# Third and fourth pair of the first group on POOL, and another pair order in down's first column groups

## The chip, the cores and the metric

The kernel runs on one core of one Trainium2 chip, in one launch. The metric is the device time of the program in microseconds (us), lower is better; the kernel before was run three times (2105.24, 2107.07 and 2103.96 us, median 2105.24). Profiles are taken by the hardware profiler from one execution. The engines are PE (TensorE), DVE (VectorE), ACT (ScalarE), POOL (GpSimd) and SP (SyncE, which here only issues DMAs).

## The reference

One layer of a streaming encoder on a residual stream x of 256 rows by 2048 columns, float32:

```python
x = x + 1/2 * SwiGLU_1(RMSNorm(x))     # d_ff 5504
h = RMSNorm(x); P = h @ W_in           # one combined projection
m = sigmoid(g_gdn) * (gated_deltanet(P) @ W_A) + sigmoid(g_att) * (chunk_attention(P) @ W_B)
x = x + m @ W_out
x = x + 1/2 * SwiGLU_2(RMSNorm(x))

def swiglu(h, w_gate, w_up, w_down):
    return (jax.nn.silu(h @ w_gate) * (h @ w_up)) @ w_down
```

Nearly all of the time is in matrix products of the 256 rows with weights that are read once from memory, 408 MB in all. The two SwiGLU blocks (gate and up, then down) hold the largest share of them.

## The kernel before, in words

Every float32 number is held as a high part (rounded by a cast to the PE's type fp32r) and a low part (the rest), and every product is three matmuls: high by high, high by low, low by high (lines 455, 456 and 457, in `product`). Weights come by DMA as f32 (`raw`, two DMAs of 512 KB for one pair), ACT casts the high part (`wh`, line 373) and DVE subtracts for the low part (`wl`, line 427). PE's matmuls name what they read, so "pf<-wl,xr" is the product with the low weights.

The work goes by pairs of k tiles (256 rows of a weight). Function `seven` computes one column group from eight pairs. A pair is either plain (24 matmuls) or fast: seven products in place of eight for the 2x2 blocks of a pair (21 matmuls), for which DVE first makes four sums of weight blocks (`s`, lines 399 to 401), ACT casts them (`sh`, line 406) and DVE subtracts (`sl`); the blocks that are used as they are become `w` and `v` (line 404). A fast pair so costs PE three matmuls less and DVE three times as much as a plain one. Its products go to seven banks in PSUM, numbered by bits (1, 2, 3, 4, 5, 6, 7, 8 in the names, "pd_00_4"); at the end of a column group they are added into four results, copied out (`ed`, lines 524 to 537) and, for down, added to the residual in memory by a DMA from POOL's queue (line 621).

Weights are planned ahead as one list (`plan`); `take_weights` draws from it in the order in which the products use them, and the order of the instructions on each engine is set by the scheduler of the framework from the order in the code. The order on each engine is fixed when the program is built, and an engine works through its own queue in that order.

Two places matter here. In the first column group of the first FFN, x itself arrives while the weights do. The pairs come in the order FIRST = 1, 3, 5, 7, 0, 2, 4, 6; pairs 1, 3, 5 and 7 are plain, the others fast in later groups. `feed(s)` runs ahead of step s: it loads x of pair FIRST[s+2], scales x of pair FIRST[s+1] by the norm's weight and splits it (`Xr.plain`: per pair two scalings with a cast on ACT, line 180, and two subtractions on DVE, line 181), and at given steps calls `stand(k4)`: eight transposes of x on PE (line 1142), two copies from PSUM, squares for the norm, and a store of the rows to memory (`put`, line 649).

The other place is down (hidden to 2048 columns). For two of the three chunks of each FFN, the 16 k tiles of the chunk are eight pairs, and `seven` runs them in order 0 to 7 for two column groups of 1024 columns (d = 0 and d = 2); pairs 2, 3, 5 and 6 (DEEP) are fast, so that 2 and 3 and later 5 and 6 stand side by side. Two chunks in each of two FFNs make four such places.

## Time and profile before

| | |
|---|---|
| median of three runs | 2105.24 us (2103.96 to 2107.07) |
| the profiled execution | 2104.86 us |
| its span in the trace | 2103.1 us |
| PE busy | 2086.8 us, 99% of the span |
| DVE, ACT, POOL busy | 1798.9, 1190.7 and 64.5 us |
| mean granted TensorE clock | 0.999 |
| memory read, written | 407.72 MB, 25.17 MB |

The span is what the profiler sees from the first to the last instruction; the run's own time is 1.8 us longer. PE is busy nearly throughout, so a time can only get shorter where PE idles or works slowly. The profile lists for each group of instructions the idle time just before it and what ended that time; such an entry on PE is the place to look.

### The profile page before, as it was taken

To read this page: it belongs to the slowest core of one execution; us is meant where nothing else is said; L and a number is where in the kernel's file an instruction comes from. 1 tells how busy PE (TensorE), PEld (TensorE's weight loads), DVE (VectorE), ACT (ScalarE), POOL (GpSimd) and SP (SyncE) were. 2 spreads that over 40 slices of the span, in tenths; PEclk is the share of its full clock that TensorE was granted. 3 is DMA by queue.
4 is the path that set the end of the run, shared out by engine and by line. 5 is a ranking of instruction groups with operands and counts; after the bars stand their busy time and mean duration, and the time that the engine had idled before them with its cause. 6 is when DMAs were issued, how large, how long until landed. Compare 5 with 4: busy or idle time off the path is not lost.

```text
span 2103.1 us, 25704 instructions
## 1 busy us (share of the span) xinstructions
PE 2086.8 (99%) x9732; PEld 1743.5 (83%) x9732; DVE 1798.9 (86%) x2015; ACT 1190.7 (57%) x1226; POOL 64.5 (3%) x77
## 2 busy tenths in 40 slices
PE   8999999999999999999999999999999999999999
PEld 6888888878898988888888888888887888878897
DVE  6998999989996688767785787999999999989982
ACT  6755565646555555557545555556555555556561
POOL 0000110002000000000010000000000100011000
PEclk9999999999999999999999999999999999999999
DMA  9655995649866656435454466767665975579581
GB/s 314 218 188 177 261 266 196 207 145 278 257 212 219 238 187 224 163 127 197 145 175 159 151 200 220 230 203 228 207 193 169 276 243 192 180 207 294 188 271 60
DMA packets 398204, 434.59 MB, mean 207 GB/s; under 512 B 14704, under 2 KB 372352, under 8 KB 397824
## 3 DMA queue, kind: packets, MB, share of 16 engines
q1 hardware_dynamic: 388864, 416.17, 60.8%
q0 software_dynamic: 9216, 16.78, 4.5%
q8 instruction: 76, 1.25, 0.3%
q14 instruction: 48, 0.39, 0.1%
HBM read 407.72 MB, written 25.17 MB: 206 GB/s over the span
## 4 chain that ended last, share of the span: by engine, by line
PE 95%; DVE 2%; SPq 1%; issue 1%; DMA 0%; ACT 0%; DVEq 0%; ACTq 0%
PE pf L455 14%; PE pf L457 14%; PE pf L456 14%; PE pd L456 7%; PE pd L457 7%; PE pd L455 7%; PE pg L456 2%; PE pg L457 2%; PE pg L455 2%; PE pc L455 2%; PE pc L457 2%; PE pc L456 2%; PE pwo L455 1%; PE pwo L457 1%; PE pwo L456 1%; DVE wl L427 1%
## 5 line engine op out<-in xcount | busy, mean ns | idle before, releaser
L427 DVE TENSOR_TENSOR wl<-raw,wh 128x2048 fp32r<-128x2048 f32 (+5 forms) x278 | 587.2, 2120 | 69.6 <-PE pc L456 17.0
L373 ACT CAST wh<-raw 128x2048 fp32r<-128x2048 f32 (+5 forms) x278 | 490.2, 1779 | 95.3 <-DVE wl L427 18.3
L406 ACT CAST sh<-s 128x2048 fp32r<-128x2048 f32 (+1 forms) x123 | 233.0, 1894 | 292.5 <-DVE s L401 288.4
L427 DVE TENSOR_TENSOR sl<-s,sh 128x2048 fp32r<-128x2048 f32 (+1 forms) x123 | 276.9, 2257 | 27.3 <-PE pd L456 12.0
L456 PE MATMUL pf<-wl,xr 128*128 128x512 f32 (+1 forms) x704 | 271.4, 386 | 0.2 <-DVE wl L427 0.2
L457 PE MATMUL pf<-wh,xr 128*128 128x512 f32 (+1 forms) x704 | 271.0, 385 | 0.0
L455 PE MATMUL pf<-wh,xr 128*128 128x512 f32 (+1 forms) x704 | 263.3, 387 | 3.9 <-ACT xr L180 2.4
L457 PE MATMUL pd<-wh,hid 128*128 128x512 f32 x432 | 169.1, 391 | 0.0
L456 PE MATMUL pd<-wl,hid 128*128 128x512 f32 x432 | 168.3, 390 | 0.0
L404 ACT CAST w<-raw 128x1024 fp32r<-128x1024 f32 (+1 forms) x123 | 128.0, 1041 | 65.4 <-DVE sl L427 12.8
L455 PE MATMUL pd<-wh,hid 128*128 128x512 f32 x432 | 163.6, 392 | 0.0
L455 PEld LDWEIGHTS pf<-wh,xr 128*128 128x128 f32 x704 | 132.4, 188 | 30.3 <-ACT wh L373 2.9
L427 DVE TENSOR_TENSOR w<-raw,w 128x1024 fp32r<-128x1024 f32 (+1 forms) x123 | 148.1, 1204 | 10.4 <-ACT w L404 10.2
L399 DVE TENSOR_TENSOR s<-raw 128x1024 f32<-128x1024 f32 (+1 forms) x123 | 147.9, 1202 | 7.1 <-PE pg L456 4.6
L456 PEld LDWEIGHTS pf<-wl,xr 128*128 128x128 f32 x704 | 132.6, 188 | 25.3 <-DVE wl L427 0.5
L457 PEld LDWEIGHTS pf<-wh,xr 128*128 128x128 f32 x704 | 132.6, 188 | 25.3
L404 ACT CAST v<-raw 128x512 fp32r<-128x512 f32 (+1 forms) x123 | 75.6, 615 | 97.0 <-PE pf L457 32.3
L456 PE MATMUL pf<-sl,xf 128*128 128x512 f32 (+1 forms) x292 | 112.3, 385 | 0.0
L457 PE MATMUL pf<-sh,xf 128*128 128x512 f32 (+1 forms) x292 | 112.0, 385 | 0.0
L455 PE MATMUL pf<-sh,xf 128*128 128x512 f32 (+1 forms) x292 | 110.2, 386 | 0.0
L621 POOL DMA_DIRECT2D xd<-ed x64 | 56.0, 996 | 1305.5 <-ACT ed L524 1225.5
L457 PEld LDWEIGHTS pd<-wh,hid 128*128 128x128 f32 x432 | 81.1, 188 | 17.2
(509 smaller groups left out, 4270.5 us busy)
## 6 DMA issues: line engine op xcount, KB each, us to landing
raw<-wd SPq DMA_DIRECT2D x168, 512.0 KB, 5.2
raw<-wg SPq DMA_DIRECT2D x159, 512.0 KB, 3.8
raw<-wu SPq DMA_DIRECT2D x159, 512.0 KB, 5.3
raw<-wgt SPq DMA_DIRECT2D x64, 512.0 KB, 4.6
raw<-wa SPq DMA_DIRECT2D x48, 512.0 KB, 4.6
raw<-wc SPq DMA_DIRECT2D x48, 512.0 KB, 4.7
xd<-ed POOLq DMA_DIRECT2D x64, 256.0 KB, 7.0
raw<-wbr SPq DMA_DIRECT2D x32, 512.0 KB, 5.2
```

Source lines behind the costliest of these rows:

```text
L373: nc.scalar.copy(hi, src)
L399: nc.vector.tensor_sub(S[:, 0:2], R[:, 1], R[:, :, 0])
L404: nc.scalar.copy(hi, src)
L406: nc.scalar.copy(sh, s)
L427: nc.vector.tensor_sub(lo, src, f32(hi))
L455: nc.tensor.matmul(dst, ah, wh, start=start, stop=False)
L456: nc.tensor.matmul(dst, ah, wl, start=False, stop=False)
L457: nc.tensor.matmul(dst, al, wh, start=False, stop=stop)
L621: b: lambda e, dst=xd[d + dd][t]: nc.gpsimd.dma_start(dst, e, accum_op=ALU.add)
```

## The change

Three things change. In the first group, x of the third and fourth pair (5 and 7) is scaled and split by a new function `Xr.pool` on POOL: two multiplications of 128x256, a cast of 128x512 and a subtraction of 128x512 for each pair, through a scratch tile `xa`. The steps in which `stand` is called each move one later, those of the last two falling together: steps 5, 6, 7 and 7 in place of 4, 5, 6 and 7. And down's first column groups (d = 0) take their pairs in the order APART = 0, 1, 2, 4, 3, 7, 5, 6, in the plan of the weights as in `seven`; the fast ones are still 2, 3, 5 and 6.

```diff
@@ -32,6 +32,7 @@
 DOWN = (2, 4, 6)
 SECOND = (1, 3, 0, 2, 4, 5, 6, 7)
 DEEP = (2, 3, 5, 6)
+APART = (0, 1, 2, 4, 3, 7, 5, 6)
 FIRST = (1, 3, 5, 7, 0, 2, 4, 6)
 QUAD = {2: (0, 0), 3: (1, 0), 4: (0, 1), 8: (1, 1)}
 CHUNKS = ((0, 4), (4, 8), (8, 11))
@@ -180,6 +181,16 @@
                 nc.scalar.activation(hi, src(i), AF.Copy, scale=self.w(j, i))
                 nc.vector.scalar_tensor_tensor(lo, src(i), self.w(j, i), f32(hi), op0=ALU.mult, op1=ALU.subtract)
 
+        def pool(self, j, src):
+
+            b = self.place(j)
+            a = wide(f"xa{self.nm}{j}").rearrange("p (b x) -> p b x", x=P)
+            for i in range(2):
+                to = a[:, 2 * i : 2 * i + 2].rearrange("p t x -> p (t x)")
+                nc.gpsimd.tensor_scalar_mul(to, src(i), self.w(j, i))
+            nc.gpsimd.tensor_copy(b[:, 0, 0:4], a)
+            nc.gpsimd.tensor_sub(b[:, 1, 0:4], a, f32(b[:, 0, 0:4]))
+
         def scale(self, j, src, a):
             for i in range(2):
                 nc.scalar.activation(
@@ -285,10 +296,11 @@
                     for j, p in zip(js, gu):
                         yield j in fast_pairs(f, i), p
                 k0, k1 = FG[a0][0], sum(FG[a1 - 1])
-                cols = lambda d: t_pieces(a["wd" + f], 4 * d, 4, k0, k1)
+                cols = lambda d, js=None: t_pieces(a["wd" + f], 4 * d, 4, k0, k1, js and [k0 + 2 * j for j in js])
                 if down_pairs(a0, a1):
                     for d in (0, 2):
-                        yield from sevens(cols(d), cols(d + 1), DEEP)
+                        js = range(KD // 2) if d else APART
+                        yield from sevens(cols(d, js), cols(d + 1, js), DEEP, js)
                 else:
                     for d in range(4):
                         yield from twos(cols(d))
@@ -300,8 +312,8 @@
         for p in pieces:
             yield False, (p, next(pieces))
 
-    def sevens(one, two, fast=DOWN):
-        for j, pieces in enumerate(zip(one, two)):
+    def sevens(one, two, fast=DOWN, pairs=range(KD // 2)):
+        for j, pieces in zip(pairs, zip(one, two)):
             yield j in fast, pieces
 
     def mixing():
@@ -621,7 +633,7 @@
                         b: lambda e, dst=xd[d + dd][t]: nc.gpsimd.dma_start(dst, e, accum_op=ALU.add)
                         for b, (dd, t) in QUAD.items()
                     }
-                    seven(f"d{nm}_{a0}{d}", 512, fast, block, out=out)
+                    seven(f"d{nm}_{a0}{d}", 512, fast, block, pairs=range(KD // 2) if d else APART, out=out)
                 continue
             for d in range(4):
                 pd = pair(f"pd{nm}_{a0}{d}")
@@ -1156,7 +1168,7 @@
     def feed(s):
 
         if s < 7:
-            xr1.plain(FIRST[s + 1], pair_of_x(FIRST[s + 1]))
+            (xr1.pool if 0 < s < 3 else xr1.plain)(FIRST[s + 1], pair_of_x(FIRST[s + 1]))
         if s < 6:
             load_x(2 * FIRST[s + 2], 2)
         if s == 1:
@@ -1166,7 +1178,7 @@
         if s > 1 and FIRST[s] in xr1.fast:
             xr1.more(FIRST[s], pair_of_x(FIRST[s]))
         for k4 in range(4):
-            if s == max(3, *(FIRST.index(2 * k4 + i) for i in range(2))):
+            if s == min(7, 1 + max(*(FIRST.index(2 * k4 + i) for i in range(2)))):
                 stand(k4)
         if s == 7:
             xr1.finish()
```

What this does to the queues, at three places. ACT in the first group of the kernel before, from the weights of the third pair on; `wh_191` is the fourth pair's high weights, `xr_5_196` holds x of the third and then of the fourth pair, `xT` is x as loaded:

```order
L373 CAST wh_168<-raw_126 128x1024 x2
L373 CAST wh_191<-raw_158 128x2048
L180 ACTIVATE xr_5_196<-xT_81,vec 128x256 x2
L373 CAST wh_218<-raw_165 128x2048
L180 ACTIVATE xr_5_196<-xT_81,vec 128x256 x2
L373 CAST wh_237<-raw_188 128x2048
```

And after the change, ACT, and then POOL at its start:

```order
L385 CAST wh_168<-raw_126 128x1024 x2
L385 CAST wh_191<-raw_158 128x2048
L385 CAST wh_219<-raw_165 128x2048
L385 CAST wh_238<-raw_188 128x2048
L385 CAST wh_263<-raw_216 128x2048
L181 ACTIVATE xf_0_279<-xT_80,vec 128x256 x2
```

```order
L190 ISA
L190 TENSOR_SCALAR xa_197<-xT_81,vec 128x256 x2
L191 CAST xr_5_196<-xa_197 128x512
L192 TENSOR_TENSOR xr_5_196<-xa_197,xr_5_196 128x512
L190 TENSOR_SCALAR xa_242<-xT_81,vec 128x256 x2
L191 CAST xr_5_196<-xa_242 128x512
L192 TENSOR_TENSOR xr_5_196<-xa_242,xr_5_196 128x512
```

The two scalings of `xr_5_196` have left ACT, where each stood between two casts of weights, and stand on POOL with nothing but each other; the two subtractions on DVE have gone as well.

DVE in down's first column groups (first FFN, first chunk) before. `wl_1646` is pair 4's low weights; `sl_1554` and the rows of number 1545 belong to fast pair 3, `s`, `v` and `w` with 1691 to 1693 to fast pair 5:

```order
L427 TENSOR_TENSOR sl_1554<-s_1545,sh_1553 128x2048
L145 TENSOR_TENSOR shid_3_1579_0_1615<-shid_3_1579_0_1615,hid_3_1579_0_0_1608 128x128
L146 TENSOR_TENSOR shid_3_1579_0_1615<-shid_3_1579_0_1615,hid_3_1579_0_0_1608 128x128
L147 TENSOR_TENSOR shid_3_1579_0_1615<-hid_3_1579_0_0_1608,shid_3_1579_0_1615 128x128
L148 TENSOR_TENSOR shid_3_1579_0_1615<-hid_3_1579_0_0_1608,shid_3_1579_0_1615 128x128
L427 TENSOR_TENSOR v_1693<-raw_1542,v_1693 128x512
L129 TENSOR_TENSOR hs_25_1255<-shid_3_1579_0_1615,hs_25_1255 128x512
L399 TENSOR_TENSOR s_1691<-raw_1542 128x1024
L427 TENSOR_TENSOR w_1692<-raw_1542,w_1692 128x1024
L400 TENSOR_TENSOR s_1691<-s_1691,raw_1542 128x512
L401 TENSOR_TENSOR s_1691<-raw_1542,s_1691 128x512
L427 TENSOR_TENSOR wl_1646<-raw_1488,wh_1645 128x2048
```

And after the change. `wl_1548` is pair 4's low weights, `s_1639`, `w_1640` and `sl_1648` belong to fast pair 3:

```order
L146 TENSOR_TENSOR shid_3_1573_0_1609<-shid_3_1573_0_1609,hid_3_1573_0_0_1602 128x128
L147 TENSOR_TENSOR shid_3_1573_0_1609<-shid_3_1573_0_1609,hid_3_1573_0_0_1602 128x128
L148 TENSOR_TENSOR shid_3_1573_0_1609<-hid_3_1573_0_0_1602,shid_3_1573_0_1609 128x128
L149 TENSOR_TENSOR shid_3_1573_0_1609<-hid_3_1573_0_0_1602,shid_3_1573_0_1609 128x128
L130 TENSOR_TENSOR hid_3_1573<-hid_3_1573_2_0_1629,hid_3_1573 128x2x256
L130 TENSOR_TENSOR hs_25_1257<-shid_3_1573_0_1609,hs_25_1257 128x512
L411 TENSOR_TENSOR s_1639<-raw_1490 128x1024
L412 TENSOR_TENSOR s_1639<-s_1639,raw_1490 128x512
L439 TENSOR_TENSOR w_1640<-raw_1490,w_1640 128x1024
L413 TENSOR_TENSOR s_1639<-raw_1490,s_1639 128x512
L439 TENSOR_TENSOR wl_1548<-raw_1452,wh_1547 128x2048
L439 TENSOR_TENSOR sl_1648<-s_1639,sh_1647 128x2048
```

Pair 4's subtraction has moved ahead of `sl` of pair 3, and the sums of pair 5 no longer stand in front of it.

ACT at the end of the same column groups before, from the first casts for the next column group on (`ed_00_2` to `ed_00_8` are the copies of banks 2, 3, 4 and 8; `v` and `w` with 1843, 1844, 1870 and 1871 are weights of d = 2):

```order
L524 COPY ed_00_0_1823<-pd_00_1_1663 128x512
L373 CAST wh_1835<-raw_1753 128x2048
L404 CAST v_1844<-raw_1795 128x512
L537 COPY ed_00_2_1896<-pd_00_2_1580 128x512
L404 CAST v_1871<-raw_1832 128x512
L537 COPY ed_00_3_1900<-pd_00_3_1594 128x512
L404 CAST w_1843<-raw_1795 128x1024
L537 COPY ed_00_4_1904<-pd_00_4_1584 128x512
L537 COPY ed_00_8_1908<-pd_00_8_1598 128x512
L406 CAST sh_1850<-s_1842 128x2048
```

And after the change (1885, 1886 and 1901 are weights of d = 2):

```order
L385 CAST wh_1789<-raw_1709 128x2048
L385 CAST wh_1831<-raw_1757 128x2048
L536 COPY ed_00_0_1856<-pd_00_1_1663 128x512
L416 CAST v_1886<-raw_1786 128x512
L416 CAST w_1885<-raw_1786 128x1024
L416 CAST v_1901<-raw_1828 128x512
L549 COPY ed_00_2_1866<-pd_00_2_1574 128x512
L549 COPY ed_00_3_1870<-pd_00_3_1588 128x512
L549 COPY ed_00_4_1874<-pd_00_4_1578 128x512
L549 COPY ed_00_8_1878<-pd_00_8_1592 128x512
```

The copies of the four banks are still behind two casts of `v`; banks 2 and 3 no longer have a cast between them.

## Rows read from the trace of the kernel before

**Rows 1.** The page's part 1: busy time of each engine, its share of the span and its instructions.

```profile
span 2103.1 us, 25704 instructions
...
PE 2086.8 (99%) x9732; PEld 1743.5 (83%) x9732; DVE 1798.9 (86%) x2015; ACT 1190.7 (57%) x1226; POOL 64.5 (3%) x77
```

**Rows 2.** What PE waited for over the whole span: us in total, times, the longest one.

```profile
PE pd L455 <- ACT sh L406: 3.7, 4, 0.9
PE pf L455 <- ACT xr L180: 2.4, 1, 2.4
```

**Rows 3.** PE by the time, end of the second and start of the third pair of the first group: start us, duration us, engine, line, operation, names, shapes, count, and in brackets the idle time before it with what ended it.

```profile
18.62 0.39 PE L457 MATMUL pf<-wh,xr 128*128 128x512 f32 x1
21.42 0.72 PE L455 MATMUL pf<-wh,xr 128*128 128x512 f32 x1 [2.41 <-ACT xr L180]
...
24.93 0.41 PE L457 MATMUL pf<-wh,xr 128*128 128x512 f32 x1
```

**Rows 4.** The first group in stretches of 5 us: busy time and instructions of PE, PEld, DVE, ACT and POOL, then the granted TensorE clock, the DMA share and GB/s.

```profile
20.00:25.00 5.00, 3.58 (x9) 2.84 (x10) 3.08 (x3) 3.66 (x4) 0.00 (x0) 0.66 1.09 359
...
30.00:35.00 5.00, 4.70 (x23) 3.65 (x22) 1.48 (x1) 2.09 (x3) 0.00 (x0) 1.00 1.09 355
```

**Rows 5.** ACT by the time in the first group, columns as in rows 3.

```profile
19.06 1.90 ACT L373 CAST wh<-raw 128x2048 fp32r<-128x2048 f32 x1 [2.72 <-DMA raw<-wu]
20.86 0.90 ACT L180 ACTIVATE xr<-xT,vec 128x256 fp32r<-128x256 f32 x2
22.06 1.90 ACT L373 CAST wh<-raw 128x2048 fp32r<-128x2048 f32 x1 [0.29 <-DMA raw<-wu]
25.65 0.91 ACT L180 ACTIVATE xr<-xT,vec 128x256 fp32r<-128x256 f32 x2 [1.70 <-DMA xT<-x]
...
34.56 0.91 ACT L180 ACTIVATE xf<-xT,vec 128x256 fp32r<-128x256 f32 x2 [2.91 <-DMA xT<-x]
```

**Rows 6.** The load of x for the third pair, which SP issues at 7.83 us (line 84): its time to landing; then the chain of waits at the fifth pair: start, us, what.

```profile
DMA to landing us min/median/max: 8.1/8.1/8.1
...
24.39 10.09 DMA xT<-x
```

**Rows 7.** DVE by the time in the first group.

```profile
22.20 2.28 DVE L427 TENSOR_TENSOR wl<-raw,wh 128x2048 fp32r<-128x2048 f32 x1
...
27.00 4.49 DVE L427 TENSOR_TENSOR wl<-raw,wh 128x2048 fp32r<-128x2048 f32 x2
```

**Rows 8.** PE by the time, end of the fourth pair, the first eight transposes and the fifth pair.

```profile
33.83 0.39 PE L457 MATMUL pf<-wh,xr 128*128 128x512 f32 x1
34.52 1.09 PE L1142 MATMUL xs<-cst,xT 128*128 128x128 f32 x8 [0.30 <-DMA xT<-x]
35.37 0.48 PE L455 MATMUL pf<-wh,xf 128*128 128x512 f32 x1
```

**Rows 9.** POOL's own computing, by the time, in the mixing stage.

```profile
1075.93 1.81 POOL L966 MEMSET gdn_pk<- 128x2048 f32 x1 [544.44 <-DVE wl L427]
1077.81 0.43 POOL L968 COPY gdn_pk<-gdn_E 32x256 f32<-32x256 f32 x1
...
1095.39 0.61 POOL L968 COPY gdn_pk<-gdn_E 64x512 f32<-64x512 f32 x1
```

**Rows 10.** DVE beside the second of those rows.

```profile
1077.79 0.19 DVE L976 TENSOR_TENSOR gdn_ls<-gdn_lw,gdn_ls 128x16 f32<-128x16 f32 x1
```

**Rows 11.** PE by the time in down's first column groups, first FFN, first chunk.

```profile
208.03 1.07 PE L455 MATMUL pd<-wh,hid 128*128 128x512 f32 x4
...
209.16 0.39 PE L456 MATMUL pd<-w,hid 128*128 128x512 f32 x1
209.39 0.39 PE L457 MATMUL pd<-w,hid 128*128 128x512 f32 x1
210.71 0.74 PE L455 MATMUL pd<-sh,hs 128*128 128x512 f32 x2 [0.93 <-ACT sh L406]
```

**Rows 12.** DVE by the time at the same place.

```profile
200.04 2.29 DVE L427 TENSOR_TENSOR sl<-s,sh 128x2048 fp32r<-128x2048 f32 x1 [1.17 <-PE pd L457]
...
203.41 0.69 DVE L427 TENSOR_TENSOR v<-raw,v 128x512 fp32r<-128x512 f32 x1 [0.17 <-ACT v L404]
...
204.63 1.22 DVE L399 TENSOR_TENSOR s<-raw 128x1024 f32<-128x1024 f32 x1
205.76 1.22 DVE L427 TENSOR_TENSOR w<-raw,w 128x1024 fp32r<-128x1024 f32 x1
...
207.61 0.69 DVE L401 TENSOR_TENSOR s<-raw,s 128x512 f32<-128x512 f32 x1
208.22 2.28 DVE L427 TENSOR_TENSOR wl<-raw,wh 128x2048 fp32r<-128x2048 f32 x1
```

**Rows 13.** ACT by the time at the same place.

```profile
208.76 1.90 ACT L406 CAST sh<-s 128x2048 fp32r<-128x2048 f32 x1
```

**Rows 14.** Two weight loads of down (line 350, two DMAs each), the first issued at 207.5 to 208.0 us, the second at 221.3 to 221.7: their time to landing.

```profile
DMA to landing us min/median/max: 3.8/4.4/4.9
...
DMA to landing us min/median/max: 6.1/6.6/7.1
```

**Rows 15.** ACT by the time where down's first column groups are carried out of the banks.

```profile
228.85 0.62 ACT L404 CAST v<-raw 128x512 fp32r<-128x512 f32 x1 [1.57 <-DMA raw<-wd]
229.41 0.59 ACT L537 COPY ed<-pd 128x512 f32<-128x512 f32 x1
```

## The prediction

> **What bounds the kernel now.** I read the busy times first: PE works 2086.8 of 2103.1 us [rows 1], so only PE's waits and slow stretches can be won, some 16 us. Next the list of what PE waited for. Its largest entry is in down: 3.7 us in four waits of 0.9 us, for the cast of a fast pair's sums on ACT. Its next is a single wait of 2.4 us for x in the first group [rows 2]. The change is aimed at both, so I followed each in the time lines.
>
> In the first group PE issues the last matmul of the second pair at 18.62 and the first of the third at 21.42 [rows 3]. A matmul follows the one before in 0.23 us (209.16 to 209.39 in [rows 11]), so PE could have started at 18.85 and lost 2.57 us. What it waited for stands on ACT: x of the third pair is scaled at 20.86, right behind a cast of weights that began at 19.06 after 2.72 us of waiting for a DMA [rows 5]. That x was issued at 7.83 and landed 8.1 us later, at 15.95 [rows 6]: it lay ready for nearly 5 us behind a cast that it doesn't need. After the gap PE is slow: eight matmuls take 21.42 to 24.93, 3.51 in place of 8 x 0.23 = 1.84 us, and the granted clock averages 0.66 over that stretch [rows 3, 4]. Gap and slow matmuls together are 2.57 + 1.67 = 4.2 us.
>
> Now the limit behind it. In these stretches the DMA share is 1.09 [rows 4]: transfers are full and land in the order of issue. x of the fourth pair is there at 25.65, x of the fifth (pair 0) at 24.39 + 10.09 = 34.48 [rows 5, 6]. PE issues the last matmul of the fourth pair at 33.83, starts eight transposes at 34.52, when x of pair 0 is in, and pair 0 at 35.37 [rows 8].
>
> In down, PE issues the last product with `w` at 209.39 and the next, with `sh`, at 210.71 [rows 11]. Behind that `sh` cast (ACT, 208.76, 1.90 long [rows 13]) the queue of DVE shows why all is late: `wl` of the plain pair 4 runs from 208.22 to 210.50, behind `sl` of pair 3 (200.04, after 1.17 us for a free slot) and behind `v`, `s` and `w` of fast pair 5 [rows 12]. The wait is booked to `sh`, but PE needs both.
>
> **The change part by part.** The first part is POOL. It takes from ACT two scalings per pair (0.91 us) and from DVE two subtractions. On POOL the trace shows no multiplication and no two-input operation. The nearest rows are copies of 32x256 in 0.43 and of 64x512 in 0.61 us, and a memset of 128x2048 in 1.81 [rows 9]. I take 0.43 for a multiplication, 0.61 for the cast, and an estimated 1.2, twice the copy, for the subtraction with two inputs; the ends are 0.43 to 0.61 and 1.81 for any of the four. The Trainium skill (GPSIMD Engine Reference, section 3.1) gives 4497 ns for a two-input addition of 2048 elements there; a quarter of that, as an estimate, is 1.12 us, and the sum would not change by it.
>
> Third pair: the high part is there at 15.95 + 0.43 + 0.43 + 0.61 = 17.4, the low one at 18.6; PE wants them at 18.85 and 19.3. So that gap closes, and the pair ends at 18.85 + 24 x 0.23 = 24.4. But the fourth pair's x comes at 25.65 all the same: high part at 27.1, low part at 28.3. PE idles 2.7 us there, about as long as before, and I charge the same slow matmuls, 1.67 us. The third matmul wants the low part at 27.1 + 0.9 = 28.0 and gets it 0.3 late. The pair ends at 27.1 + 5.5 + 1.7 + 0.3 = 34.6.
>
> Pair 0 cannot gain from this. Its x lands at 34.48, ACT begins the two scalings at 34.56 and takes 0.91 for both [rows 5], so the first half, which the first matmul reads, is ready at about 35.1. By the order of the program five of the first `stand`'s eight transposes still stand in front of pair 0, at 1.09 / 8 = 0.11 apart from the tail (34.52 to 35.37) [rows 8]; they end at 34.6 + 0.55 = 35.15. Pair 0 starts at 35.13, against 35.37: 0.24 us won, and three transposes of 0.11 come later, 0.33 lost. The first group is worth **+0.1 us**: the 4.2 us are not won but moved to the fourth pair, since x of pair 0 sets the end. The moved `stand`s add nothing else; all 32 transposes are there before and after, and the stores that they issue on SP go behind weight loads that are early. With every POOL operation at 1.81 the fourth pair's parts come at 31.1 and 32.9, it ends at about 39.2, and pair 0 starts at 39.7: +4.3 + 0.33 = +4.7 us. There is no slack, so each further microsecond on POOL's chain costs one. The low end is the +0.1 itself.
>
> Second part, down. With pair 4 ahead of pair 3, `sl` of pair 3 with its slot wait (2.29 + 1.17), `v` (0.69) and the sums of pair 5 (1.22 + 1.22 + 0.68 + 0.69 = 3.81) no longer stand in front of `wl`: it would end at 210.50 - 7.96 = 202.5. Walking DVE's and ACT's queues of the new program row by row, with these durations and the slots that each waits for, I get 204.1. PE wants it after the four `wh` products that make way at 208.94 (209.16 - 0.23 in [rows 11]), less one fast pair of 21 x 0.23 = 4.8: at 204.2. So the margin is 0.1 to 1.7 us. The same walk gives margins of 0.4 us at pair 7's `wl`, 0.2 at `sl` of pair 5, 1.6 at pair 6's and 2.8 at the next column group's first `wl`. A fast pair costs DVE 6.8 us (3.81, 0.69, 2.29) against 4.8 on PE, a plain one 2.29 against 5.5, so the pair set between the fast ones is what gives DVE its time back. I take the stall as gone: 210.71 - 209.39 - 0.23 = 1.09 us at each of four places, **-4.36 us**. Bounds: nothing gone (0), or a new stall, priced below. PE has no idle time behind these places that could absorb it.
>
> Sum: -4.36 + 0.1 = -4.26. The profiled execution took 2104.86 us (span 2103.1 and 1.8 around it), so 2100.6; the median of the runs is 0.38 higher, which makes **2101.0 us**. A measurement tells about 0.2%, 4.2 us, from no change, so the forecast lies on that edge, at 2101.03.
>
> **Rivals.** A: POOL and DVE hold each other up. The only row with both at work, a copy of 0.43 at 1077.81 beside a DVE operation of 0.19 [rows 9, 10], is too short to tell. If a long two-input DVE operation excludes a reading POOL one, the `wl` behind the cast of 22.06 to 23.96 runs to 26.24 [rows 5, 7], 0.6 past the landing of the fourth x, and the next `wl`, which can start from about 26 on, may take 2.28 between two of POOL's operations. High and low part then come about 2.3 us later, pair 0 starts near 37.4: 2103.3, and 2104 with both. The Trainium skill (SBUF — State Buffer, Who interferes with whom) says that a DVE instruction with two inputs in SBUF contends with a GpSimd instruction that reads SBUF, the one waiting for the whole of the other; no row here shows it.
>
> B: the stalls in down stay in part, since margins of 0.1 to 0.4 us are thin: 0.3 to 0.7 us left at each place, 2102.2 to 2103.8.
>
> C, slower: the handover to d = 2. The last pair is now fast, so the banks are copied out at the very end of the group, and on ACT these copies stand behind a cast of `v` whose weights are loaded last. By the walk they are issued at 223.3; such loads landed after 4.9 us in one place and 7.1 in another [rows 14], and in the latter the cast did wait, 1.57 us, with the copy behind it [rows 15]. At 4.9: landed 228.2, cast 0.62, copy 0.59, ready 229.5, and PE wants the bank at 229.7. At 7.1: ready at 231.6, 1.9 us lost at each of four places, 7.6 in all: 2108.6. It outweighs the gain from a landing of about 6.3 us on. Against it: the 7.1 us were behind a load issued 1.2 us earlier; here the one before is some 4 us older.
>
> D: POOL is slow, 1.81 us and more for each operation: 2105.6.
>
> **How the numbers follow.** The forecast has a chance of 0.55, with a range of its own of 2099.8 to 2102.3; A 0.14, B 0.10, C 0.11, D 0.10. The forecast falls beyond the 0.2% in somewhat over six of ten, which makes faster 0.36; the rest of it with A, B and most of D is the same, 0.50; C and a little of D are slower, 0.14. The range for 8 in 10 takes in A, B and D and leaves out C and the lowest tail: 2099.5 to 2106.
>
> **What would show it.** PE's list without the four waits for `sh` in down; `wl` of pair 4 on DVE ending some 4 us before its place now; the third pair's first matmul at 18.85 at full clock; a gap of nearly 3 us at the fourth pair, released by POOL; pair 0 at 35.1. The forecast is wrong if pair 0 starts after 36 (A or D: look at POOL's durations), or if PE waits at the start of d = 2 for ACT's copies (C), or if pair 0 comes well before 35, which would say that x landed earlier.

## The result, and the profile after

The changed kernel takes 2113.68 us (median of six runs, 2111.71 to 2114.08), the kernel before beside it 2105.71 us (six runs); the ratio is 1.0034, with a 95% interval of 1.0024 to 1.0044. It is slower by some 7 us, where 4.3 us less were forecast. In the profiled execution the span is 2109.9 us, 6.8 more than before. PE's own work is the same 9732 matmuls; 6.0 of the 6.8 us are counted as busy, since slow matmuls and the short delays of a matmul behind a wait count as busy [rows 1]:

```profile
span 2109.9 us, 25723 instructions
...
PE 2092.8 (99%) x9732; PEld 1742.5 (83%) x9732; DVE 1799.5 (85%) x2011; ACT 1188.1 (56%) x1222; POOL 75.2 (4%) x85
```

What PE waited for after the change, columns as in [rows 2]:

```profile
PE pf L467 <- POOL xr L191: 5.1, 2, 4.9
...
PE pd L467 <- ACT sh L418: 1.2, 4, 0.3
...
PE pd L467 <- ACT ed L549: 1.1, 4, 0.5
...
PE pf L469 <- POOL xr L192: 0.8, 2, 0.6
```

The two entries of [rows 2] are gone or smaller, and three have come: POOL's cast with 5.1 us, POOL's subtraction with 0.8, and the bank copies in down with 1.1. The wait for `sh` fell from 3.7 to 1.2, but these are other places than before (below).

The first group, POOL by the time; the rows of POOL that there were before are [rows 9]:

```profile
15.70 2.34 POOL L190 TENSOR_SCALAR xa<-xT,vec 128x256 f32<-128x256 f32 x2 [15.26 <-DMA xT<-x]
18.11 0.61 POOL L191 CAST xr<-xa 128x512 fp32r<-128x512 f32 x1
18.81 1.28 POOL L192 TENSOR_TENSOR xr<-xa,xr 128x512 fp32r<-128x512 f32 x1
25.28 4.35 POOL L190 TENSOR_SCALAR xa<-xT,vec 128x256 f32<-128x256 f32 x2 [5.19 <-DMA xT<-x]
29.70 0.61 POOL L191 CAST xr<-xa 128x512 fp32r<-128x512 f32 x1
30.40 1.28 POOL L192 TENSOR_TENSOR xr<-xa,xr 128x512 fp32r<-128x512 f32 x1
```

The cast takes 0.61 and the subtraction 1.28 us, as estimated. The two multiplications take 2.34 us for the third pair and 4.35 for the fourth, where 0.86 was forecast. DVE over the second of these, to be read beside [rows 7]:

```profile
23.56 2.29 DVE L439 TENSOR_TENSOR wl<-raw,wh 128x2048 fp32r<-128x2048 f32 x1 [0.73 <-ACT wh L385]
26.55 2.29 DVE L439 TENSOR_TENSOR wl<-raw,wh 128x2048 fp32r<-128x2048 f32 x1 [0.70 <-ACT wh L385]
```

DVE's subtractions run from 23.56 to 25.85 and from 26.55 to 28.84. POOL's multiplications begin at 25.28 and end, one by one, at 26.64 and 29.63: each ends 0.79 us after a DVE instruction has ended. PE, to be read beside [rows 3] and [rows 8]:

```profile
18.78 0.50 PE L467 MATMUL pf<-wh,xr 128*128 128x512 f32 x1 [0.21 <-POOL xr L191]
...
20.14 0.51 PE L469 MATMUL pf<-wh,xr 128*128 128x512 f32 x1 [0.63 <-POOL xr L192]
...
25.05 0.39 PE L469 MATMUL pf<-wh,xr 128*128 128x512 f32 x1
30.36 0.73 PE L467 MATMUL pf<-wh,xr 128*128 128x512 f32 x1 [4.93 <-POOL xr L191]
...
31.73 0.79 PE L469 MATMUL pf<-wh,xr 128*128 128x512 f32 x1 [0.21 <-POOL xr L192]
...
37.85 0.71 PE L1154 MATMUL xs<-cst,xT 128*128 128x128 f32 x5
38.31 0.48 PE L467 MATMUL pf<-wh,xf 128*128 128x512 f32 x1
```

The third pair starts at 18.78 at full clock; the forecast said 18.85, but PE was free at 18.40 in this execution and lost 0.38 us there and 0.80 more at the low part. The fourth starts at 30.36, 5.3 us after the third pair's last matmul, and pair 0 at 38.31, against 35.37 in [rows 8]. The stretches of 6 us show the clock that went with it:

```profile
24.00:30.00 6.00, 1.44 (x7) 0.86 (x5) 4.14 (x2) 2.65 (x2) 4.65 (x3) 1.00 1.08 362
30.00:36.00 6.00, 5.43 (x16) 3.94 (x17) 2.39 (x6) 4.22 (x6) 1.59 (x2) 0.72 1.09 357
```

PE did 1.44 us of work from 24 to 30, and from 30 to 36 its granted clock averaged 0.72, as it did over 20 to 25 before with 0.66 [rows 4].

Down, first place. PE does not wait at pair 4 any more, but starts d = 2 behind a bank copy, and waits for `sh` in d = 2, at pair 5, where it did not wait before:

```profile
234.09 0.50 PE L467 MATMUL pd<-wh,hid 128*128 128x512 f32 x1 [0.19 <-ACT ed L549]
...
255.52 0.73 PE L467 MATMUL pd<-sh,hs 128*128 128x512 f32 x2 [0.32 <-ACT sh L418]
```

ACT, to be read beside [rows 15]: the cast of `v` comes at 232.93 (before: 228.85; 3.2 of these 4.1 us are the later start of down), and the four bank copies right behind it. The cast of `w` ahead of it had waited 1.17 us for a slot that PE still read:

```profile
231.67 1.06 ACT L416 CAST w<-raw 128x1024 fp32r<-128x1024 f32 x1 [1.17 <-PE pd L468]
232.93 0.62 ACT L416 CAST v<-raw 128x512 fp32r<-128x512 f32 x1 [0.20 <-DMA raw<-wd]
233.46 2.04 ACT L549 COPY ed<-pd 128x512 f32<-128x512 f32 x4
```

To see where 6.8 us come from, I cut the span at the first matmul of each product (start times of PE's rows). The last two columns are experiments 1 and 2 below. Between before and after only these stretches differ by more than 0.1 us:

| stretch, us | before | after | APART alone | POOL part alone |
|---|---|---|---|---|
| first gate and up chunk, with the first group | 180.4 | 184.0 | 180.0 | 184.7 |
| down, four places | 85.4, 85.4, 85.4, 85.5 | 85.9, 86.2, 86.0, 86.0 | 86.0, 85.9, 85.7, 86.8 | 85.4, 86.2, 85.4, 85.4 |
| gate and up behind each of them | 166.4, 114.1, 166.4, 114.1 | 166.6, 114.4, 166.6, 114.3 | 166.6, 114.3, 166.6, 114.3 | 166.4, 114.1, 166.4, 114.1 |

The first stretch lost 3.6 us, the four places in down 0.5 to 0.9 each, and the chunks behind them another 0.2 to 0.3 each: 3.6 + 2.6 + 1.0 us, less 0.35 by which the first matmul came earlier in this execution.

### The profile page after: what moved, and what is told of

Read it like the earlier page. It is cut to its first block, busy times and chain, and to the rows that moved or that the text cites. A ratio compares the mean times of both kernels' runs of the same rounds, so it can differ in the third digit from the quotient of the medians.

```text
span 2109.9 us, 25723 instructions
## 1 busy us (share of the span) xinstructions
PE 2092.8 (99%) x9732; PEld 1742.5 (83%) x9732; DVE 1799.5 (85%) x2011; ACT 1188.1 (56%) x1222; POOL 75.2 (4%) x85
## 4 chain that ended last, share of the span: by engine, by line
PE 93%; DVE 3%; DMA 1%; ACT 1%; SPq 1%; issue 1%; POOL 0%; DVEq 0%; ACTq 0%
PE pf L467 14%; PE pf L469 14%; PE pf L468 14%; PE pd L468 6%; PE pd L467 6%; PE pd L469 6%; PE pg L468 2%; PE pg L467 2%; PE pg L469 2%; PE pc L467 2%; PE pc L469 2%; PE pc L468 2%; PE pwo L467 1%; PE pwo L469 1%; PE pwo L468 1%; DMA raw<-wd 1%
## 5 line engine op out<-in xcount | busy, mean ns | idle before, releaser
L469 PE MATMUL pd<-wh,hid 128*128 128x512 f32 x432 | 168.7, 390 | 0.0
L468 PEld LDWEIGHTS pd<-wl,hid 128*128 128x128 f32 x432 | 81.2, 188 | 20.3 <-DVE wl L439 4.3
```

What stands on the lines that cost most here:

```text
L468: nc.tensor.matmul(dst, ah, wl, start=False, stop=False)
L469: nc.tensor.matmul(dst, al, wh, start=False, stop=stop)
```

## Experiments

Each kernel was run beside the kernel before, on the same chip, and the ratio is to those runs. Single runs of the kernel before lay between 2103.8 and 2112.7 us, so by time alone less than about 2 us can't be told; the stretches come from one profiled execution each. "Pair 0" is the start of the first matmul of the fifth pair; it was at 35.4 before. A "slip" is by how much a matmul starts later than 0.23 us behind the one before.

**1. Down's part alone.** The changed kernel without POOL and with `stand` as before:

```diff
-            (xr1.pool if 0 < s < 3 else xr1.plain)(FIRST[s + 1], pair_of_x(FIRST[s + 1]))
+            xr1.plain(FIRST[s + 1], pair_of_x(FIRST[s + 1]))
...
-            if s == min(7, 1 + max(*(FIRST.index(2 * k4 + i) for i in range(2)))):
+            if s == max(3, *(FIRST.index(2 * k4 + i) for i in range(2))):
```

> Only the pair order APART in down's first column groups; x in the first group and the transposes stand as before. Theory 1 (the stall in down is not removed but broken up: each place gives back 1.1 us at pair 4 and loses about 2 us to small waits at pair 4's and 7's weights, at the bank copies of the handover to d = 2, and at the sums of d = 2's pair 5): about 3 to 4 us slower than before, 2108 to 2110, with the waits for ACT's bank copies (1.1 us over four) and for sh (1.2 over four) in PE's list as in the changed kernel. Rival (down's part does win about 4 us by itself, and its small waits come from the shift that POOL's part causes): 2101 to 2102, and no wait for the bank copies.

Measured: 2108.34 us, ratio 1.0013 (1.0003 to 1.0023). Down's places take 85.7 to 86.8 us, and the wait for `sh` is 1.2 us over four, as in the changed kernel; the bank copies, expected with 1.1 over four, are listed with one wait of 0.2 (their slips are 0.13 to 0.36, against 0.35 to 0.65 in the changed kernel):

```profile
PE pd L467 <- ACT sh L418: 1.2, 4, 0.3
```

At the first place the slips are, in order: 0.15 and 0.11 at pair 4's low weights, the same at pair 7's, 0.11 at the next `sl`, 0.36 and 0.11 at the bank copy, 0.11 once, 0.46 and 0.11 at `sh` in d = 2, and in the next gate and up chunk 0.19 and 0.11. Two of the 0.11 stand in the kernel before too; the rest, 1.9, is more than the one stall of 1.09 and its 0.1 behind it. The rival is out: down's part alone costs about 3 us (0.6 to 4.8 by the interval).

**2. POOL's part alone**, with the later transposes: the changed kernel with `range(KD // 2)` in both places of APART.

```diff
-                        js = range(KD // 2) if d else APART
+                        js = range(KD // 2)
...
-                    seven(f"d{nm}_{a0}{d}", 512, fast, block, pairs=range(KD // 2) if d else APART, out=out)
+                    seven(f"d{nm}_{a0}{d}", 512, fast, block, out=out)
```

> POOL's part and the later transposes alone; down's pairs in the old order. Theory 1 (POOL's two multiplications wait for DVE's long subtractions, and nothing gives it back): pair 0 starts at about 38, 3 us later than before, and the time is 3 to 3.6 us above before, 2108.5 to 2109.5; the four waits for sh of 0.9 us in down are back. Rival (most of the loss stems from down, and the first group costs only what a shift costs): 2105 to 2106.

Measured: ratio 1.0028 (1.0017 to 1.0039), pair 0 at 39.3, the first stretch 4.3 us longer than before, both more than expected: behind the same gap of 4.9 us the granted clock averaged 0.52 from 30 to 36, against 0.72 in the changed kernel. PE's waits:

```profile
PE pf L467 <- POOL xr L191: 5.2, 2, 4.9
PE pd L467 <- ACT sh L418: 3.7, 4, 0.9
```

So the loss has two parts, by the trace 4.3 us in the first group here and 3 to 4 us in experiment 1, and each is made where its part of the change is.

**3. The transposes alone.** The kernel before with `stand` one step later.

```diff
-            if s == max(3, *(FIRST.index(2 * k4 + i) for i in range(2))):
+            if s == min(7, 1 + max(*(FIRST.index(2 * k4 + i) for i in range(2)))):
```

> Only the transposes of x one step later; x scaled on ACT and DVE as before, down in the old order. Theory 1: five transposes still fill the gap before pair 0, three come later: pair 0 starts at 35.1 to 35.2, the time is within 0.5 us of before. Rival (the moved transposes themselves cost, since they no longer fill a gap): 0.9 us above before or more.

Measured: ratio 0.9996 (0.9987 to 1.0004), pair 0 at 35.3 with five transposes ahead of it. The first stretch is 180.7 us long against 180.4, which fits the 0.33 that the sum had for them; the run times can't tell so little.

**4. DVE's subtractions cut.** The changed kernel, with this in `prepare`, for the weights of the fourth to sixth pair:

```diff
-            nc.vector.tensor_sub(lo, src, f32(hi))
+            for at in range(0, 1024, 256):
+                q = slice(at, at + 256)
+                nc.vector.tensor_sub(lo[:, :, q], src[:, :, q], f32(hi[:, :, q]))
```

> The changed kernel, with DVE's three long subtractions for the weights of the fourth, fifth and sixth pair cut into four of 128x512 each (about 0.65 us each in place of 2.29). Theory 1 (a POOL operation that reads waits until the running DVE instruction with two inputs has ended, whatever its length): the fourth pair's two multiplications take 2 to 3 us in place of 4.35, PE's wait for POOL's cast falls from 4.9 to 3 to 3.8 us, and the time falls by 1 to 2 us against the changed kernel, to 2111.5 to 2112.5. Rival (the multiplications are slow by themselves, 1.2 to 2.2 us each, whatever DVE does): 4.3 us as before, and the changed kernel's time.

Measured: ratio 1.0027 (1.0017 to 1.0037), not told apart from the changed kernel's by time. POOL and DVE:

```profile
25.93 3.27 POOL L190 TENSOR_SCALAR xa<-xT,vec 128x256 f32<-128x256 f32 x2 [5.20 <-DMA xT<-x]
29.27 1.10 POOL L191 CAST xr<-xa 128x512 fp32r<-128x512 f32 x1
```

```profile
24.22 2.50 DVE L442 TENSOR_TENSOR wl<-raw,wh 128x512 fp32r<-128x512 f32 x4 [0.53 <-ACT wh L385]
27.20 2.69 DVE L442 TENSOR_TENSOR wl<-raw,wh 128x512 fp32r<-128x512 f32 x4 [0.48 <-ACT wh L385]
```

The multiplications fell from 4.35 to 3.27 us, short of the 2 to 3 expected, the cast rose to 1.10, and PE's wait for it fell only from 4.9 to 4.4. The four pieces of 24.22 to 26.72 follow each other without a gap, and POOL's first multiplication, begun at 25.93, ended at 27.43, 0.71 behind the last of them: it was not let in between them. The second, of 1.79 us, was let in after two pieces, and the third piece then took 0.88 us in place of 0.68. So it is DVE's running work that holds POOL, but cutting it freed POOL in one of two cases.

**5. Loads of x one step earlier, with POOL's part** (down in the old order):

```diff
-        if s < 6:
-            load_x(2 * FIRST[s + 2], 2)
+        for n in range(s + 2 + (s > 0), min(s + 4, 8)):
+            load_x(2 * FIRST[n], 2)
```

> POOL's part and the later transposes as changed, down in the old order, and x of the fourth and all later pairs loaded one step earlier, ahead of weights that are needed later. Theory 1 (POOL's chain takes 5 to 6.5 us, and cost time because it could begin only when x of the fourth pair had landed): POOL now begins the fourth pair behind the third, at about 20 us, and is ready at 25 to 26; PE's wait for POOL's cast falls from 5 to under 1 us, pair 0 starts at 32 to 33 in place of 38 to 39, and the time is 2 to 3 us below before. Rival (POOL beside DVE's subtractions is what costs, wherever it stands): the wait stays at 3 us or more, time at or above before.

Measured: ratio 1.0004 (0.9996 to 1.0013), pair 0 at 35.7. POOL and DVE:

```profile
15.97 4.14 POOL L190 TENSOR_SCALAR xa<-xT,vec 128x256 f32<-128x256 f32 x4 [15.53 <-DMA xT<-x]
20.07 1.17 POOL L191 CAST xr<-xa 128x512 fp32r<-128x512 f32 x2
21.21 4.55 POOL L192 TENSOR_TENSOR xr<-xa,xr 128x512 fp32r<-128x512 f32 x2
```

```profile
21.51 3.10 DVE L439 TENSOR_TENSOR wl<-raw,wh 128x2048 fp32r<-128x2048 f32 x1 [4.00 <-ACT wh L385]
```

This does not tell the theories apart as meant: with both x there, the scheduler put all four multiplications ahead of both casts, so the third pair came late (20.7). But it gives the prices. With DVE idle from 17.5 on, a multiplication takes 0.92 us, a cast 0.61, a subtraction 1.26. The second subtraction took 3.3 us (4.55 in all), beside DVE's 2.29 us of work; and DVE's own instruction took 3.10 in place of 2.29, since POOL's first subtraction was at work when it began. Each holds up the other, and who comes first goes on.

**6. The earlier loads alone** (same edit in the kernel before).

> The kernel before with x of the fourth and all later pairs loaded one step earlier, scaled on ACT and DVE. Theory 1 (the gap at the third pair stems from ACT's order, not from the load of x): the gap of 2.4 to 2.6 us for xr stays, now for both pairs at once, and the gap before pair 0 goes: 0 to 0.7 us below before. Rival (landings of x are the limit everywhere): 2 us or more below before.

Measured: ratio 1.0002 (0.9994 to 1.0011), a wait for `xr` of 3.2 us at the third pair, pair 0 at 35.4. The third pair's gap is ACT's order, as [rows 5] had it, and loads alone win nothing.

**7. POOL's pairs one after the other.** As 5, with one scratch tile for both pairs, so that the fourth pair's multiplications wait for the third pair's subtraction.

```diff
-            a = wide(f"xa{self.nm}{j}").rearrange("p (b x) -> p b x", x=P)
+            self.scratch = getattr(self, "scratch", None) or wide(f"xa{self.nm}{j}").rearrange("p (b x) -> p b x", x=P)
+            a = self.scratch
```

> As pool_xearly, but both pairs share one scratch tile on POOL, so that POOL finishes the third pair before it begins the fourth. Theory 1 (a POOL multiplication takes 0.8 to 0.9 us by itself, and what costs is the start after x's landing and DVE's subtractions in the way): the third pair starts at 18.5 to 19.2 as in the changed kernel, the fourth pair's cast on POOL ends at 24 to 25.5 and PE waits for it 1 us at most; pair 0 starts at 32 to 33.5, then held by ACT's order, 2 to 3 us below before. Rival (POOL's work delays DVE's subtractions in turn, and the weights of the fourth pair come late): a wait for wl of 1 us or more appears there, time not below before.

Measured: ratio 1.0004 (0.9995 to 1.0012). The third pair started at 19.7, the fourth at 26.1, with no wait for POOL's cast and 0.6 us for its subtraction; so POOL can do this work in time if it has x early. The cast beside DVE's subtraction took 2.10 us in place of 0.61. And yet pair 0 starts only at 34.7:

```profile
22.91 2.10 POOL L192 CAST xr<-xa 128x512 fp32r<-128x512 f32 x1
```

```profile
31.61 1.03 PE L1155 MATMUL xs<-cst,xT 128*128 128x128 f32 x8
34.53 0.41 PE L1155 MATMUL xs<-cst,xT 128*128 128x128 f32 x2 [1.88 <-DMA xT<-x]
```

PE had done the fourth pair at 31.6 and then stood for x of the sixth pair, which two transposes ahead of pair 0 read. The first stretch is 179.1 us long in this execution, 1.3 less than before, and down's first place 86.9, 1.5 more, with a cast of `v` that waited 3.98 us for its weights as in experiment 12.

**8. The same on DVE, without POOL.** Loads as in 5; x of the third and fourth pair is scaled by DVE, which idles there (the multiplications take 0.3 us each):

```diff
+        def dve(self, j, src):
+            b = self.place(j)
+            for i in range(2):
+                hi, lo = (b[:, s, 2 * i : 2 * i + 2, :].rearrange("p t x -> p (t x)") for s in range(2))
+                nc.vector.tensor_scalar_mul(hi, src(i), self.w(j, i))
+                nc.vector.scalar_tensor_tensor(lo, src(i), self.w(j, i), f32(hi), op0=ALU.mult, op1=ALU.subtract)
...
-            xr1.plain(FIRST[s + 1], pair_of_x(FIRST[s + 1]))
+            (xr1.dve if 0 < s < 3 else xr1.plain)(FIRST[s + 1], pair_of_x(FIRST[s + 1]))
```

> The kernel before with x of the fourth and later pairs loaded one step earlier, and x of the third and fourth pair scaled on DVE (which idles there) in place of ACT. Theory 1 (the gap at the third pair is ACT's order alone): the wait for xr goes, the third pair starts before 19.3 at full clock, no half-clock matmuls up to 30 us, pair 0 at 32 to 33.5, held by ACT's cast of weights ahead of its x: 2 to 3 us below before. Rival (the DMA's landings hold PE in any case): pair 0 at 35, no gain.

Measured: ratio 1.0005 (0.9996 to 1.0014). Both gaps are gone: third pair at 18.4, fourth at 23.8, its end at 29.3, 4.8 us ahead of before. And then:

```profile
29.29 1.04 PE L1150 MATMUL xs<-cst,xT 128*128 128x128 f32 x8
33.77 0.41 PE L1150 MATMUL xs<-cst,xT 128*128 128x128 f32 x2 [3.44 <-DMA xT<-x]
```

Pair 0 starts at 33.9, behind a gap of 3.4 us; eight of its matmuls run at half speed (0.43 us apart), and the first stretch is 180.7 us long, against 180.4. All that was won at the third and fourth pair was lost at the fifth: theory 1 holds for the gap at the third pair, the rival for the time.

**9. x of the third to fifth pair on DVE, x of the fifth and sixth pair loaded together** (against 8):

```diff
-            (xr1.dve if 0 < s < 3 else xr1.plain)(FIRST[s + 1], pair_of_x(FIRST[s + 1]))
-        for n in range(s + 2 + (s > 0), min(s + 4, 8)):
+            (xr1.dve if 0 < s < 4 else xr1.plain)(FIRST[s + 1], pair_of_x(FIRST[s + 1]))
+        for n in {0: (2, 3), 1: (4, 5), 2: (6,), 3: (7,)}.get(s, ()):
```

> As x_dve, with x of the fifth pair (pair 0) scaled on DVE too, and x of the fifth and sixth pair loaded together, ahead of weights. Theory 1 (once the third and fourth pair no longer wait, PE's next wait is for x of the sixth pair, which transposes ahead of pair 0 read, and for ACT's order): pair 0 starts at 31 to 32, without a gap of 3.4 us before it, the first phase is 3 to 4.5 us shorter than before. Rival (the DMA is full, so what is loaded earlier makes weights late): a new wait for weights of 1 us or more within the first 60 us, less than 1.5 us won.

Measured: ratio 1.0011 (1.0002 to 1.0019), pair 0 at 35.2. The transposes no longer wait, and x of pair 0 landed at 26.65, but DVE's scaling of it (34.69) stands in the queue behind two subtractions of weights (30.28 to 34.76), which stand behind small sums that waited 1.91 us for ACT:

```profile
PE pf L463 <- DVE xf L188: 3.7, 1, 3.7
```

The theory's 31 to 32 failed; the new wait is again one of order. One place in down took 88.3 us in this run: the cast of `v` waited 5.4 us for its weights there, as in experiment 12 below.

**10. Pair 5 plain in d = 0** (kernel before, `fast` without 5 in d = 0 in the plan and in `seven`).

```diff
-                        yield from sevens(cols(d), cols(d + 1), DEEP)
+                        yield from sevens(cols(d), cols(d + 1), DEEP if d else tuple(j for j in DEEP if j != 5))
...
-                    seven(f"d{nm}_{a0}{d}", 512, fast, block, out=out)
+                    seven(f"d{nm}_{a0}{d}", 512, fast if d else [j for j in fast if j != 5], block, out=out)
```

> The kernel before with pair 5 plain in down's first column groups (fast: 2, 3, 6), fast as before in d = 2: in each of four places 3 matmuls more on PE (0.68 us) and 4.5 us less on DVE. Theory 1 (from about 200 us to the end of down DVE is busy throughout, so a stall that is only moved comes back; less DVE work removes it): the four waits for sh are gone and none takes their place, 4 x (0.68 - 1.09 - 0.2) = 1.6 to 2.6 us below before. Rival (queue order and slots make the stall, not DVE's work): a wait of 0.5 us or more stays at each place, 1 to 2.7 us above before.

Measured: 2104.58 us, ratio 0.9993 (0.9985 to 1.0002). The four waits for `sh` are gone, and four waits for `wl` of 0.2 to 0.3 us have come:

```profile
PE pd L456 <- DVE wl L427: 0.9, 4, 0.3
```

Down's places take 85.5, 85.2, 85.2 and 85.1 us, the three added matmuls (0.68) included: 0.6 us won in all, less than the 1.6 to 2.6 expected, and not told from before by time.

**11. 8 with 10, and 9 with 10.**

> x_dve and three together. If both hold, their gains add: 4 to 5.5 us below before, clearly faster. Rival (a gain in the first group is given back at the first place where DVE or the DMA is behind, some 200 us later): no more than three alone.

> x_dve4 with pair 5 plain in down's first column groups. If the gains add, 3.5 to 5 us below before, 2100 to 2101.5. Rival: no more than 2 us below before, since what is won in the first group is lost again by late weights.

Measured: 0.9997 (0.9988 to 1.0006) and 0.9992 (0.9982 to 1.0001). Neither beats the kernel before clearly, as the rivals had it; pair 0 stood at 34.3 and 34.6.

**12. Other pair orders in d = 0.** The changed kernel without its part in the first group (as in experiment 1), with another order:

```diff
-APART = (0, 1, 2, 4, 3, 7, 5, 6)
+APART = (0, 2, 1, 3, 4, 5, 6, 7)
```

> Only down's first column groups in another order, 0, 2, 1, 3, 4, 5, 6, 7 (2, 3, 5 and 6 fast): the last pair is plain again, and 5 and 6 stand together as in the kernel before. Theory 1 (the handover's waits for bank copies come from a fast last pair, the wait at d = 2's pair 5 from two fast pairs at the end): neither shows; the stall at pair 4 may stay or go: 0 to 4 us below before. Rival (any other order than 0 to 7 upsets d = 2): the wait in d = 2 at pair 5 of about 0.5 us stays, and the time is above before.

Measured: ratio 1.0000 (0.9990 to 1.0010). The stall at pair 4 is back with its 0.9 us at each place, and d = 2 has no wait for `sh`; three places took 85.4 to 85.7 us. With the last pair plain there are no waits behind it, as theory 1 said. The first place took 88.0 us, by what rival C of the prediction describes, in a kernel that does not have a fast last pair, and as a single event:

```profile
232.26 0.62 ACT L416 CAST v<-raw 128x512 fp32r<-128x512 f32 x1 [5.03 <-DMA raw<-wd]
```

The cast of `v` waited 5.03 us for its weights, bank copies stood behind it, and PE waited at d = 2's start (0.69 us for a copy, then 1.30 for `wl`).

**13. Fast and plain in turn** (DEEP = 0, 2, 4, 6, kernel before otherwise):

```diff
-DEEP = (2, 3, 5, 6)
+DEEP = (0, 2, 4, 6)
```

> The kernel before with pairs 0, 2, 4 and 6 of down taken by seven products in place of 2, 3, 5 and 6, in order 0 to 7, in both column groups: fast and plain alternate and the last pair is plain. Theory 1 (the stalls in down come from two fast pairs in a row, 13.6 us of DVE against 9.6 on PE): no wait for sh above 0.2 us in the four places, none for the bank copies, 3 to 5 us below before. Rival (what counts is how early in the group the fast pairs come, since DVE arrives late from the gate and up products): a new wait at the first pair of each place, before's time or above.

Measured: ratio 1.0045 (1.0033 to 1.0057), with sixteen waits for `sh`:

```profile
PE pd L455 <- ACT sh L406: 7.2, 16, 0.9
PE pf L455 <- ACT sh L406: 2.5, 1, 2.5
```

Theory 1 fell here: there are four waits at each place, of its eight fast pairs. Counted by the same matmuls as in the table, a place takes 87.1 to 87.4 us, 1.8 to 2.0 more than before: the five matmuls that experiment 14 speaks of stand behind down here too, and their 1.13 us are put back. That fits a view in which DVE gets ahead only in a run of plain pairs, and there is none, but doesn't show it. The other 4.9 us were lost in the first gate and up chunk, which this edit was not meant to touch: on ACT the copy of a bank now stands ahead of the cast of a fast pair's sums, which followed it at 119.31, and PE waited 2.5 us for that:

```profile
118.83 0.58 ACT L524 COPY ef<-pf 128x512 f32<-128x512 f32 x1 [8.16 <-PE pf L457]
```

**14. APART in both column groups** (against 1):

```diff
-                        js = range(KD // 2) if d else APART
+                        js = APART
...
-                    seven(f"d{nm}_{a0}{d}", 512, fast, block, pairs=range(KD // 2) if d else APART, out=out)
+                    seven(f"d{nm}_{a0}{d}", 512, fast, block, pairs=APART, out=out)
```

> Pair order APART in both column groups of down (d = 0 and d = 2), x and transposes as before. Theory 1 (DVE is busy throughout from d = 0's end to the next gate and up products, so the lag that APART leaves it with shows at the next fast pair, wherever it stands): the wait for sh at d = 2's pair 5 (0.48 us slip) goes, but a wait of 0.3 us or more shows at the end of d = 2 or at the first fast pair of the next gate and up group, and the phase from down's start to that group stays 0.5 us or more above before. Rival (it is the place of pair 4 behind pair 3 in d = 2): the phase falls to 85.4 us, as before, or below.

Measured: ratio 1.0035 (1.0025 to 1.0045). Cut as in the table, down's places take 84.5, 84.5, 85.2 and 84.8 us and the gate and up chunks behind them 168.7 and 116.5, which looks like 0.9 won and 2.4 lost. But the cut doesn't hold here. In the kernel before, five matmuls of the next chunk run inside down's place (266.35 to 267.49 at the first), and with APART in both groups all stand behind it:

```profile
266.35 0.39 PE L455 MATMUL pf<-w,xf 128*128 128x512 f32 x1
```

With these 1.13 us put back, the places take 85.6, 85.6, 86.3 and 85.9 us, 0.2 to 0.9 more than before, and the chunks 167.6 and 115.3 to 115.4, 1.2 to 1.3 more. Nothing was won in down. The wait for `sh` at d = 2's pair 5 is gone, as theory 1 had it, four waits for `sl` of up to 0.3 us stand at the end of d = 2, and the larger part is paid at the first pairs of the next chunk; the rival is out.

**15. APART in d = 0 with pair 5 plain** (1 with the edit of 10):

> APART in d = 0 with pair 5 plain there (fast 2, 3, 6): 4.5 us less on DVE, 0.68 us more on PE at each place. Theory 1 (the waits of APART come from DVE's and ACT's lag): the waits at d = 2's pair 5 and in the next gate and up group go, the phases fall from 85.9 to 86.2 us to about 85.2, near the kernel before. Rival (they come from the order, that is from a fast last pair and the bank copies behind it): phases of 85.8 us or more, with the waits for the bank copies at 0.3 us or more each.

Measured: ratio 1.0017 (1.0008 to 1.0026). The waits for bank copies are gone; the wait for `sh` in d = 2 is not, its slip is 0.58 in place of 0.46 us at the first place:

```profile
PE pd L467 <- ACT sh L418: 3.7, 4, 1.8
```

(the longest, 1.8 us, is at the fourth place, where matmuls at half speed follow it; that place took 88.7 us, the others 85.9 to 86.5, with 0.68 for the added matmuls in each; three of the four chunks behind are still 0.2 to 0.3 longer). So, the single events of 7, 9 and 12 apart, the bank copies waited only where two fast pairs stood side by side at the end; that ACT and DVE are late there for that reason was not tested further. The wait in d = 2 did not go with DVE's work in d = 0, and theory 1 fell for that half.

## Why the prediction was wrong

**What bounds the kernel: right.** Both stalls were read rightly. Gap and slow matmuls at the third pair are gone when x is scaled elsewhere (18.8 in the changed kernel, 18.4 with DVE), and the cause was ACT's order, not the load (experiments 6 and 8). The claim that pair 0 sets the end is borne out well beyond the change: in all kernels where POOL is not late pair 0 starts between 33.9 and 35.7, whether the fourth pair began at 23.8 or at 29.3. What holds it is not always its own x, though: with x loaded earlier it was x of the sixth pair in 7 and 8, and DVE's order in 9.

**POOL: the step that failed first is the price of the multiplications and of what holds them up**, in "I take 0.43 for a multiplication". By itself one takes 0.92 us, not 0.43 (two of them: 1.0 us more); the cast (0.61) and the subtraction (1.26 to 1.28 against 1.2) were right. The larger part is rival A. The fourth pair's multiplications began when DVE was at work and waited 0.57 us for one DVE subtraction and 2.2 for the next. From x's landing to the high part took 5.1 us, where 1.5 were counted; "there is no slack, so each further microsecond on POOL's chain costs one" then did the rest: 3.6 us on the first stretch. A was given 0.14 and a price of 2.3 us for one lost turn; its mechanism was right, its price too low by the multiplications' own 1.0. The Trainium skill (SBUF — State Buffer, Who interferes with whom) had the rule, and the rows here agree on POOL's side: 4.35 us beside DVE's subtractions, 1.83 without, in experiments 5 and 7; on DVE's side they differ from it, for DVE was held for less than the whole of POOL's operation (last section). The prediction had it as a rival, since no row of before showed it; the words "no row here shows it" are not a reason for a low chance.

**Down: the failed step is "I take the stall as gone ... PE has no idle time behind these places that could absorb it".** The stall of 1.09 at pair 4 did go, but the margins walked were not there: PE slips 0.15 at pair 4's `wl`, where 0.1 to 1.7 to spare were counted (208.94 less 4.83 is 204.1, not 204.2, so by the walk's own terms the low end was nothing), and 0.15 at pair 7's, where 0.4 were. Each slip has 0.11 behind it, so some 0.5 us a place stayed, which is rival B's case.

What failed further is the view that nothing follows. Part of it is rival C's place, the bank copies behind the cast of `v`, but hardly its mechanism: the load landed after 5.05 us, as in the better row of [rows 14], and the cast waited 0.20 for it; it was issued, in the time of before, about 1.3 us later than walked, since the slot that it needs came free later, and the cast of `w` ahead of it waited for a slot too. It cost 0.4 us and 0.1 for the restart at the first place, not 1.9. The rest was in no rival: the wait for `sh` in d = 2 and in the next gate and up chunk.

DVE's lag against PE is carried on: DVE ends the last `wl` of a place 0.42 us before PE reads it in the kernel before (267.07 and 267.49) and in 12, and 0.07 in 1 (267.51 and 267.57), where the chunk behind is 0.2 to 0.3 us longer; at the fourth place of 15, where PE had lost most, it is 0.41, and the chunk behind lost nothing. The kernel before paid 1.2 us a place for the lag, once, at d = 0; APART pays 2 in small pieces; APART in both groups pays 0.2 to 0.9 more than before in down and 1.2 behind it. That only a run of plain pairs builds up DVE's lead (7, 0, 1 in the kernel before) is what 12 to 15 point to; it was not shown by itself, for 15 took work from DVE and kept the wait.

**The transposes: right** as far as can be told (0.33 us forecast for the later three; the first stretch 0.3 longer in experiment 3).

**Sum and chances.** -4.26 was forecast. Measured by its terms: +3.6 for the first group in place of +0.1, and about +3.5 in place of -4.36 for down with what follows it. The rivals were priced one at a time; the outcome is A, B and a milder C together with one that was missing, and that sum lay outside the range.

## What to carry to other kernels

Before work is moved to POOL, look at what DVE does at that moment: a long two-input subtraction there made POOL's operation wait to its end, so that two multiplications took 4.35 us in place of 1.83, and POOL's work held DVE up in turn, by less. A stall that is removed by a new order has to be followed to the end of the next stage, with the lead of the slowest engine in the account: here a stall of 1.2 us a place came back as some 2 us of small waits. And where several things arrive late for one place, the gain from speeding up one is what the next one leaves: 4.8 us won at the fourth pair were worth 1.4 at the fifth, and nothing at the end of the chunk.

## What the runs showed that was not expected

POOL does not always get its turn between DVE instructions that follow each other without a gap: of two multiplications beside pieces of 0.6 us, one waited for the last piece, 26.72, and ended at 27.43, and one was let in between two pieces (experiment 4). DVE is held up in turn, but by less than POOL's whole operation: 0.81 us by a subtraction of 1.26 that had begun 0.30 us earlier (experiment 5), 0.18 by a multiplication of 0.92 that had begun 0.15 earlier (2.47 in place of 2.29, experiment 7). At full clock each wait of PE in the rows above, however short, cost about 0.11 us more at the next matmul, whose start then came 0.335 in place of 0.227 us after the one before.
